# A mixture-of-experts stage whose TensorE order is written out by hand and pinned

## The chip, the cores and the metric

One core of a Trainium2 chip runs the whole program. The metric is the device time of one execution in microseconds; less is better. Three executions of the kernel before are at hand, and one more was recorded by the hardware profiler.

## The reference

The program is one transformer block on 1024 tokens of width 1024: a token mixer (differential attention and gated linear attention), a layer norm, and a hierarchical mixture of experts. Only the last is touched. Each token goes to two of 32 experts:

```
def expert_block(args):
    xblk, e = args
    h = jax.nn.silu(xblk @ wg[e]) * (xblk @ wu[e])
    return h @ wd[e]
...
y = jax.ops.segment_sum(yb.astype(jnp.float32) * buf_w[:, None], buf_tok, num_segments=n_tok + 1)[:n_tok]
```

`xblk` holds 128 gathered rows of one expert; a token's two results are weighted and added. Everything is float32. An expert has three matrices of 2 MB (`wg`, `wu`, `wd`), so 192 MB of weights are read once.

## The kernel before

`experts()` runs after the mixer. Expert 0 has a fixed place (`full32`). The other 31 are sorted by how many rows they got, and rank r has a fixed room: ranks 0 to 3 have 256 rows, 4 and 5 have 192, 6 and 7 have 128, 8 to 18 have 64, and 19 to 30 have 32. Ranks 0 to 7 are called large here, the 23 others small.

**Loads.** A matrix comes in two halves of 1 MB, each by one DMA on SyncE's queue (L332) into one of eight buffers, `raw0` to `raw7` (`NRAW`, L43), which are used in turn. SyncE issues in order: a load whose buffer isn't free holds up all loads behind it.

**Large experts** (`big`, L426) split each half into a high and a low part (`split`, L336: ScalarE casts at L343, VectorE subtracts at L344), which frees the raw buffer. The parts have three buffers each. The products run in the fast fp32r form, three for each 128 rows of a half's column (`mm3`, L412; two products for a group of 64 rows, whose high and low part lie side by side): two halves of `wg`, two of `wu` (called up 0 to up 3 below), then the hidden rows are transposed (the turn, L472) and multiplied with both halves of `wd` (down, L481).

**Small experts** (`small64` L517, `small32` L554) use the raw halves as they are, in plain fp32; 64 rows fill half of the array's columns and 32 rows a quarter, so that two or four products stand side by side. Their raw buffers are free only when the products that read them are done. They too have an up, a turn (L538, L573) and a down.

**Rows** are gathered from DRAM by indirect DMAs on GpSimd's queue (L371) into two buffers (`xg`), transposed on TensorE (L380) and copied out. GpSimd's queue also issues the stores of results (L487, L551, L587), in order.

**Order.** `big`, `small64` and `small32` are generators. `chain` (L639) strings them together, and L663 to L667 take three steps of the small ones for two steps of the large ones, whatever the size of the large one; the last three small experts come behind all else (L684). This is the order in which instructions are handed to the framework. Its planner then orders each engine's instructions by its own costs, and the resulting order is fixed in the program; so products of a large and a small expert alternate in short runs on TensorE. A loop for overflowing rows (L701) runs zero times here. After it, results are gathered and normalized.

Of the kernel before, what the change touches and what calls it, by code (L numbers as in the profile page):

```python
# [74 lines left out]
class Moe:  # L75
# [232 lines left out]
    def experts(self, wg, wu, wd, g2d, out, ln2_g, ln2_b, x1d):  # L308
# [4 lines left out]
        MM = nc.tensor.matmul  # L313
# [39 lines left out]
        pxs = wx.enter_context(tc.tile_pool(name="pxs", bufs=2, reuse_waits="tile", side="right"))  # L353
# [22 lines left out]
        def x_T(xg, nm):  # L376
            for h in range(2):
                pt = ptr.tile([128, 4, 128], F32, tag="tr", name=f"tr{nm}_{h}")
                for k in range(4):
                    nc.tensor.transpose(pt[:, k, :], xg[:, (h * 4 + k) * 128:(h * 4 + k + 1) * 128], ident)  # L380
                yield slice(h * 4, h * 4 + 4), pt
# [11 lines left out]
        def x_small(u, xg=None):  # L393
            if xg is None:
                xg = gather(idx[:, u:u + 1], f"u{u}")
            T = pxs.tile([128, 8, 128], F32, tag="xT", name=f"xT{u}")
            for s, pt in x_T(xg, f"u{u}"):
                V.tensor_copy(T[:, s, :], pt)
            return T

# [11 lines left out]
        def mm3(ps, x, w, k0, nk, s=slice(0, 512)):  # L412

            for k, (wh, wl) in enumerate(w, k0):
                terms = ((x[0], wh), (x[1], wh), (x[0], wl)) if len(x) == 2 else ((x[0], wh), (x[0], wl))
                for j, (a, b) in enumerate(terms):
                    MM(ps, a[:, k, :], b[:, s], start=k + j == 0, stop=k == nk - 1 and b is wl)

# [7 lines left out]
        def big(half, xs, ydst, st=nc.gpsimd, pool=None):  # L426


            X = xs()
            n = len(X)  # L430
            w = split(half(0, 0), pool)
            yield
            ps = [[None] * n, [None] * n]
            hs = []
            order = ((0, 0), (0, 1), (1, 0), (1, 1), (2, 0))
            for j, (m, q) in enumerate(order[:4]):
                after = split(half(*order[j + 1]), pool)
                for u in range(n):
                    if q == 0:
                        ps[m][u] = pgu.tile([128, 512], F32, tag="gu", name=("pg", "pu")[m])  # L440
                    mm3(ps[m][u], X[u], w, q * 4, 8)
                w = after
                if (m, q) == (0, 1):
                    for u in range(n):
                        if len(X[u]) == 1:
                            sg = halves(ps[0][u], "sgh", "sg", 4)
                            S.activation(sg, sg, AF.Silu)
                        else:
                            sg = px.tile([128, 512], F32, tag="sg", name="sg", bufs=4)
                            S.activation(sg, ps[0][u], AF.Silu)  # L450
                        hs.append(sg)
                if j < 3:
                    yield
            w += split(half(2, 1), pool)
            hT = []
            for u in range(n):
                if len(X[u]) == 1:
                    t = halves(ps[1][u], "uph", "ys", 2)
                    V.tensor_tensor(hs[u], t, hs[u], op=ALU.mult)
                    T = px.tile([128, 4, 128], F32R, tag="hH", name="h2")  # L460
                    H, L = T[:, :, 0:64], T[:, :, 64:128]
                    hT.append((T,))
                    m = 64
                else:
                    V.tensor_tensor(hs[u], ps[1][u], hs[u], op=ALU.mult)
                    H = px.tile([128, 4, 128], F32R, tag="hH", name="hH")
                    L = px.tile([128, 4, 128], F32R, tag="hL", name="hL")
                    hT.append((H, L))
                    m = 128
                pt = ptr.tile([128, 4, m], F32, tag="tr", name="trh")  # L470
                for k in range(4):
                    nc.tensor.transpose(pt[:, k, :], hs[u][:, k * 128:(k + 1) * 128], ident[0:m, 0:m])  # L472
                S.copy(H, pt)
                V.tensor_tensor(L, pt, H.bitcast(F32), op=ALU.subtract)
            yield
            for u in range(n):
                ys = px.tile([128, 1024], F32, tag="ys", name="ys")
                for c in range(2):
                    s = slice(c * 512, c * 512 + 512)
                    yp = py.tile([128, 512], F32, tag="y", name="yp")  # L480
                    mm3(yp, hT[u], w, 0, 4, s)  # L481
                    if len(X[u]) == 1:
                        t = halves(yp, "yh", "sg", 4)
                        V.tensor_tensor(ys[0:64, s], t, g2[0:64, s], op=ALU.mult)
                    else:
                        V.tensor_tensor(ys[:, s], yp, g2[:, s], op=ALU.mult)
                st.dma_start(ydst[u], ys if len(X[u]) == 2 else ys[0:64])  # L487
            yield

        def full32(raws, T, ydst):  # L490
# [8 lines left out]
            h = px.tile([128, 512], F32, tag="sg", name="hf", bufs=4)  # L499
# [3 lines left out]
            for k in range(4):  # L503
                nc.tensor.transpose(pt[:, k, :], h[:, k * 128:(k + 1) * 128], ident)
# [4 lines left out]
            for c in range(2):  # L509
                yp = py.tile([128, 512], F32, tag="y", name="ypf")  # L510
# [6 lines left out]
        def small64(r, half, xs, c0, p0):  # L517


            T = xs()  # L520
            yield
            ps = pgu.tile([128, 512], F32, tag="gu", name=f"ps{r}")
            for k in range(8):
                if k % 4 == 0:
                    a, b = half(0, k // 4)[0], half(1, k // 4)[0]
                x = T[:, k, c0:c0 + 64]
                s = slice((k % 4) * 512, (k % 4) * 512 + 512)
                MM(ps[0:64, :], x, a[:, s], start=k == 0, stop=k == 7)  # L528
                MM(ps[64:128, :], x, b[:, s], start=k == 0, stop=k == 7)  # L529
                if k == 3:  # L530
                    yield
            sg = px.tile([128, 512], F32, tag="sg", name=f"sg{r}", bufs=4)
            S.activation(sg[64:128, :], ps[0:64, :], AF.Silu)  # L533
            h = px.tile([64, 512], F32, tag="sg", name=f"h{r}", bufs=4)
            V.tensor_tensor(h, ps[64:128, :], sg[64:128, :], op=ALU.mult)
            pt = ptr.tile([128, 4, 64], F32, tag="tr", name=f"trh{r}")
            for k in range(4):
                nc.tensor.transpose(pt[:, k, :], h[:, k * 128:(k + 1) * 128], ident[0:64, 0:64])  # L538
            hT = px.tile([128, 4, 64], F32, tag="hH", name=f"hT{r}")
            V.tensor_copy(hT, pt)  # L540
            yield
            d = [half(2, 0), half(2, 1)]
            yp = pgu.tile([128, 512], F32, tag="gu", name=f"yp{r}")
            for k in range(4):
                for c in range(2):
                    o = (k % 2) * 1024 + c * 512
                    MM(yp[c * 64:c * 64 + 64, :], hT[:, k, :], d[k // 2][0][:, o:o + 512], start=k == 0, stop=k == 3)
            ys = px.tile([128, 512], F32, tag="ys", name=f"ys{r}")
            V.tensor_tensor(ys, yp, g2h, op=ALU.mult)
            for c in range(2):  # L550
                nc.gpsimd.dma_start(yd[p0:p0 + 64, c * 512:c * 512 + 512], ys[c * 64:c * 64 + 64, :])  # L551
            yield

        def small32(r, half, xs, c0, p0, st=nc.gpsimd):  # L554
            T = xs()
            yield
            ps = pgu.tile([128, 256], F32, tag="gu", name=f"ps{r}")
            for k in range(8):
                if k % 4 == 0:
                    ab = half(0, k // 4)[0], half(1, k // 4)[0]  # L560
                x = T[:, k, c0:c0 + 32]
                for g in range(4):
                    o = (k % 4) * 512 + (g % 2) * 256
                    MM(ps[g * 32:g * 32 + 32, :], x, ab[g // 2][:, o:o + 256], start=k == 0, stop=k == 7)  # L564
                if k == 3:
                    yield
            sg = px.tile([128, 256], F32, tag="sg", name=f"sg{r}", bufs=4)
            S.activation(sg[64:128, :], ps[0:64, :], AF.Silu)
            h = px.tile([64, 256], F32, tag="sg", name=f"h{r}", bufs=4)
            V.tensor_tensor(h, ps[64:128, :], sg[64:128, :], op=ALU.mult)  # L570
            pt = ptr.tile([128, 2, 64], F32, tag="tr", name=f"trh{r}")
            for k in range(2):
# [1053 lines left out]
```

## Time and profile before

| | us |
|---|---|
| median of 3 runs | 2104.81 (2104.39 to 2104.88) |
| the profiled execution | 2098.06 |
| its span, first to last instruction | 2096.3 |
| TensorE busy in the span | 1921.5 (92%) |
| VectorE busy | 1162.1 (55%) |
| ScalarE busy | 843.0 (40%) |
| GpSimd busy | 243.7 (12%) |

A view of the trace counts microseconds from the span's start. The experts' part begins at about 1418 us, when its first weights are asked for, and the last products of a small expert start at 2032 us. Busy time of TensorE includes the drain of each product, so that isolated products count for more than their share of a dense run; the distance from one start to the next says what a product costs in a run. "DMA share" is the mean busy share of the core's 16 DMA engines, and PEclk the granted clock, 1.00 being 2.4 GHz and 0.5 being 1.2 GHz.

### The profile page before, as it was taken

What the parts mean: (1) busy time and instruction counts of PE and PEld (TensorE: products, weight loads), DVE (VectorE), ACT (ScalarE), POOL (GpSimd) and SP (SyncE); (2) the same over time, 40 slices, a digit from 0 to 9 for tenths busy, and PEclk for the clock granted to TensorE, in tenths of its full rate; (3) what the DMA queues carried; (4) which work ended last, traced back from release to release, by engine and by line L of the source; (5) the groups of instructions that cost most, each with busy time, mean ns of one, the idle gap of its engine ahead of it and who ended that gap; (6) DMA issues with size and microseconds to landing.
All of it is one profiled execution on the core that took longest, in us unless ns stands there. A gap on an engine that the chain in (4) does not pass through costs nothing. (4 is left out here: it accounts for less than half of the span.)

```text
span 2096.3 us, 29039 instructions
## 1 busy us (share of the span) xinstructions
PE 1921.5 (92%) x11039; PEld 1364.9 (65%) x11039; DVE 1162.1 (55%) x2110; ACT 843.0 (40%) x1426; POOL 243.7 (12%) x353
## 2 busy tenths in 40 slices
PE   6999999999999999999989999885998999988856
PEld 4777777777777776777767778673664555544322
DVE  7655286657665754866726567875433333444315
ACT  4322166556655663655534335331321222232202
POOL 1131100000000000000010100411111101111015
PEclk9999999999999999999999999897999999999988
DMA  7896472221123121121286735409797999999996
GB/s 270 230 249 226 159 238 66 91 91 66 56 91 94 63 91 58 61 85 57 88 269 208 244 118 201 141 31 379 303 420 288 346 371 366 349 371 404 422 386 240
DMA packets 142541, 434.32 MB, mean 207 GB/s; under 512 B 19096, under 2 KB 48408, under 8 KB 116288
## 3 DMA queue, kind: packets, MB, share of 16 engines
q1 hardware_dynamic: 98176, 350.29, 45.6%
q0 software_dynamic: 42880, 81.82, 12.2%
q8 instruction: 87, 1.43, 0.3%
q10 hardware_dynamic: 1344, 0.34, 0.1%
q14 instruction: 54, 0.44, 0.1%
HBM read 359.51 MB, written 72.89 MB: 206 GB/s over the span
## 5 line engine op out<-in xcount | busy, mean ns | idle before, releaser
L1075 DVE CUSTOM_DVE_ANT_0 t<-sc,B 128x256 f32<-128x256 f32 (+7 forms) x128 | 95.9, 754 | 63.7 <-PE sc L1072 58.6
L344 DVE TENSOR_TENSOR wL<-rawr,wH 128x1024 fp32r<-128x1024 f32 x96 | 113.8, 1219 | 15.6 <-ACT wH L343 15.3
L854 PE MATMUL v<-wv,uH 128*128 128x512 f32 x256 | 101.4, 407 | 5.0 <-DVE veL L799 2.9
L1077 ACT ACTIVATE t<-t,nm 128x256 f32<-128x256 f32 (+7 forms) x128 | 98.7, 772 | 17.2 <-DVE nm L1075 16.9
L343 ACT CAST wH<-rawr 128x1024 fp32r<-128x1024 f32 x96 | 95.2, 1046 | 23.5 <-DMA rawr<-in_wd 10.2
L816 PE MATMUL g<-uH,wH_g 128*128 128x512 f32 x256 | 102.3, 400 | 1.8 <-DVE kz L1034 1.8
L855 PE MATMUL v<-wv,uL 128*128 128x512 f32 x256 | 101.9, 398 | 0.1
L817 PE MATMUL g<-uL,wH_g 128*128 128x512 f32 x256 | 101.8, 397 | 0.0
L818 PE MATMUL g<-uH,wL_g 128*128 128x512 f32 x256 | 101.7, 397 | 0.0
L856 PE MATMUL v<-wv,uH 128*128 128x512 f32 x256 | 101.7, 397 | 0.0
L528 PE MATMUL ps<-rawr,xT 128*64 128x512 f32 x176 | 82.1, 601 | 0.6 <-DMA rawr<-in_wg 0.6
L529 PE MATMUL ps<-rawr,xT 128*64 128x512 f32 x176 | 79.2, 597 | 0.7 <-DMA rawr<-in_wu 0.7
L798 ACT CAST aH<-pta 128x512 fp32r<-128x512 f32 (+1 forms) x80 | 43.4, 542 | 71.3 <-PE pta L1096 71.0
L1070 PE MATMUL sc<-sk,sq 128*128 128x512 f32 (+2 forms) x192 | 70.2, 370 | 1.2 <-DVE nm L1075 0.3
L799 DVE TENSOR_TENSOR aL<-pta,aH 128x512 fp32r<-128x512 f32 (+1 forms) x80 | 50.7, 634 | 34.8 <-ACT aH L798 33.8
L1082 DVE SCALAR_TENSOR_TENSOR t<-t,rsum,t 128x128 f32<-128x128 f32 (+3 forms) x64 | 52.2, 816 | 27.3 <-ACT t L1081 27.0
L1072 PE MATMUL sc<-kz,sq 128*128 128x512 f32 (+2 forms) x192 | 66.0, 350 | 0.0
L564 PE MATMUL ps<-rawr,xT 128*32 128x256 f32 x768 | 56.9, 399 | 9.8 <-DMA rawr<-in_wu 7.3
L533 ACT ACTIVATE sg<-ps 64x512 f32<-64x512 f32 x11 | 6.5, 590 | 146.7 <-PE ps L529 146.7
L854 PEld LDWEIGHTS v<-wv,uH 128*128 128x128 f32 x256 | 48.1, 190 | 24.4 <-ACT ve L861 5.2
L1386 PE MATMUL wba<-baH,wH_wba 128*128 128x512 f32 x128 | 50.7, 400 | 10.8 <-DVE gs L1392 10.3
L380 PE MATMUL tru<-ident,xgu 128*128 128x128 f32 x192 | 32.3, 305 | 29.9 <-DMA xgu<-u2d,idx 26.0
(538 smaller groups left out, 5259.5 us busy)
## 6 DMA issues: line engine op xcount, KB each, us to landing
rawr<-in_wg SPq DMA_DIRECT2D x62, 1024.0 KB, 10.0
rawr<-in_wu SPq DMA_DIRECT2D x62, 1024.0 KB, 8.8
rawr<-in_wd SPq DMA_DIRECT2D x62, 1024.0 KB, 12.3
war<-in_w_ada SPq DMA_DIRECT2D x32, 512.0 KB, 5.3
yd<-o SPq DMA_DIRECT2D x24, 512.0 KB, 6.6
wa<-in_w_ada_sc SPq DMA_DIRECT2D x8, 1024.0 KB, 4.7
wvr<-in_wv SPq DMA_DIRECT2D x32, 256.0 KB, 3.0
wr_g<-in_wgt SPq DMA_DIRECT2D x16, 512.0 KB, 4.6
```

The lines of the kernel that those rows point to most:

```text
L343: S.copy(H[:, s], raw[:, s])
L344: V.tensor_tensor(L[:, s], raw[:, s], H[:, s].bitcast(F32), op=ALU.subtract)
L528: MM(ps[0:64, :], x, a[:, s], start=k == 0, stop=k == 7)
L529: MM(ps[64:128, :], x, b[:, s], start=k == 0, stop=k == 7)
L816: MM(ps, H[:, k, :], uH[k][:, s], start=k == 0, stop=False)
L817: MM(ps, H[:, k, :], uL[k][:, s], start=False, stop=False)
L818: MM(ps, L[:, k, :], uH[k][:, s], start=False, stop=k == 7)
L854: MM(ps, uH[k][:, t], wv[c][k][:, 0, :], start=k == 0, stop=False)
L855: MM(ps, uL[k][:, t], wv[c][k][:, 0, :], start=False, stop=False)
L856: MM(ps, uH[k][:, t], wv[c][k][:, 1, :], start=False, stop=k == 7)
L1075: V.tensor_tensor_reduce(out=t[:, :n], in0=ps[:, :n], in1=B[:, 1024 - n:1024], scale=1.0, scalar=3e38, op0=ALU.add, op1=ALU.min, accum_out=nm)
L1077: S.activation(t[:, :n], t[:, :n], AF.Exp, bias=nm, scale=-1.0, accum_out=rsum[:, c:c + 1])
```

## The change

Every product and transpose of `experts()` is pinned behind the one that was traced before it, so that TensorE's order is the order of the program text. `big` becomes a class whose steps (`rows`, `split`, `up`, `turn`, `down`) are called one by one; the two small forms become one class `Small`. A small expert's up is a block that stands whole between two half matrices of a large expert, with all its six loads called just ahead; its turn stands inside the large expert's next product (`mid`), and its down at the start of the next block, behind which the next small expert's rows are gathered and transposed (`small_ahead`). Large experts get four blocks (256 rows), two (192 rows) or one (128 rows), and come in the order 0, 1, 6, 4, 5, 2, 3, 7. Half k+1 is split ahead of up k. Smaller edits: small experts' sums move from the four buffers `pgu` to the two of `py`, `full32`'s from `py` to `pgu`; small rows have one buffer for each of two sizes in place of two shared; `sg` has two buffers for four; `mm3` takes the low part of the weights first.

```
-        MM = nc.tensor.matmul
+        def MM(*a, **kw):
+            return tc.keep_in_program_order(nc.tensor.matmul(*a, **kw))
+        def transpose(*a):
+            return tc.keep_in_program_order(nc.tensor.transpose(*a))
...
-        pxs = wx.enter_context(tc.tile_pool(name="pxs", bufs=2, reuse_waits="tile", side="right"))
+        pxs = wx.enter_context(tc.tile_pool(name="pxs", bufs=1, reuse_waits="tile", side="right"))
...
-                terms = ((x[0], wh), (x[1], wh), (x[0], wl)) if len(x) == 2 else ((x[0], wh), (x[0], wl))
+                terms = ((x[0], wl), (x[0], wh), (x[1], wh)) if len(x) == 2 else ((x[0], wl), (x[0], wh))
...
+        class Big:
...
+            def up(self, k, mid=lambda: None):
+                m, q = self.order[k]
+                for u, X in enumerate(self.X):
                     if q == 0:
+                        self.ps[m, u] = pgu.tile([128, 512], F32, tag="gu", name=("pg", "pu")[m])
+                    mm3(self.ps[m, u], X, self.w[k][:2], q * 4, 8)
+                    if u == 0:
+                        mid()
+                    mm3(self.ps[m, u], X, self.w[k][2:], q * 4 + 2, 8)
...
+        class Small:
...
+            def load(self):
+                self.w = {k: self.half(*k)[0] for k in ((0, 0), (1, 0), (0, 1), (1, 1), (2, 0), (2, 1))}
+            def up(self, q):
...
+                    self.ps = py.tile([128, w], F32, tag="y", name=f"ps{self.r}")
...
+        large = [r for r in (0, 1, N192, N256, N256 + 1, 2, 3, N192 + 1)]
+        small = []
+        for n in range(max(N64 - N128, NS - N64)):
+            small += [r for r in (N64 + n,) if r < NS] + [r for r in (N128 + n,) if r < N64]
...
+        def small_block():
+            nonlocal last, turned
+            cur = ahead
+            late = last and not turned
+            if late:
+                turn()
+            elif last:
+                last.down()
+            cur.load()
+            if not queue:
+                behind_loads()
+            cur.up(0)
+            if late:
+                last.down()
+            cur.up(1)
+            last, turned = cur, False
+            small_ahead()
...
+        cur = placed(large[0])
+        cur.rows()
+        small_ahead()
+        cur.split(0)
+        cur.up(0)
+        cur.split(1)
+        for n, r in enumerate(large):
+            slots = 4 if r < N256 else 2 if r < N192 else 1
+            if slots > 1 and n:
+                small_block()
+            cur.split(2)
+            cur.up(1, turn)
+            if slots > 2:
+                small_block()
+            cur.split(3)
+            cur.up(2, turn)
+            if slots > 3:
+                small_block()
+            cur.split(4)
+            cur.up(3, turn)
+            nxt = placed(large[n + 1]) if n + 1 < len(large) else None
+            if nxt:
+                nxt.rows()
+            cur.split(5)
+            if nxt:
+                nxt.split(0)
+            small_block()
+            cur.turn()
+            if nxt:
+                nxt.up(0, turn)
+            elif ahead:
+                small_block()
+            cur.down()
+            if nxt:
+                nxt.split(1)
+            cur = nxt
+        while ahead:
+            small_block()
+        turn()
+        last.down()
```

## Rows read from the trace of the kernel before

**Rows 1.** The page's 40 slices of the span: TensorE's busy tenths, and GB/s moved.

```profile
PE   6999999999999999999989999885998999988856
...
GB/s 270 230 249 226 159 238 66 91 91 66 56 91 94 63 91 58 61 85 57 88 269 208 244 118 201 141 31 379 303 420 288 346 371 366 349 371 404 422 386 240
```

**Rows 2.** Five stretches: busy us (count) per engine; the last three columns: PEclk, DMA share, GB/s.

```profile
1434.00:1461.00 27.00, 25.43 (x84) 13.16 (x82) 20.10 (x49) 4.96 (x6) 0.59 (x1) 0.97 1.02 395
1461.00:1485.00 24.00, 15.57 (x72) 10.53 (x74) 8.68 (x10) 6.24 (x8) 5.06 (x5) 0.79 0.54 198
1485.00:1575.00 90.00, 88.23 (x544) 56.10 (x540) 34.22 (x45) 23.77 (x32) 11.77 (x18) 1.00 1.01 410
1575.00:1895.00 320.00, 293.82 (x1531) 163.75 (x1531) 122.71 (x159) 78.72 (x106) 37.33 (x54) 0.96 0.91 348
1895.00:2030.00 135.00, 108.91 (x768) 51.46 (x769) 45.11 (x65) 25.81 (x33) 14.52 (x26) 0.97 1.01 418
```

**Rows 3.** DMA of 1434 to 2034 us: the sum, and the gathers, with median landing.

```profile
DMA packets 35289, 221.94 MB, mean 370 GB/s; under 512 B 4790, under 2 KB 4790, under 8 KB 11272
...
xgu<-u2d,idx POOLq DMA_INDIRECT x23, 9.3
```

**Rows 4.** Timeline of SyncE's queue around 1470 us: start, us, what.

```profile
1458.15 0.33 SPq L332 DMA_DIRECT2D rawr<-in_wu  x1
1484.43 0.33 SPq L332 DMA_DIRECT2D rawr<-in_wg  x1
```

**Rows 5.** Timeline of TensorE: the first and the third gathered row block's transposes.

```profile
1469.43 1.94 PE L380 MATMUL tru<-ident,xgu 128*128 128x128 f32 x8 [9.15 <-DMA xgu<-u2d,idx]
...
1478.86 1.04 PE L380 MATMUL tru<-ident,xgu 128*128 128x128 f32 x8
```

**Rows 6.** Timeline of GpSimd: the third gather's issue.

```profile
1471.64 0.99 POOL L371 DMA_INDIRECT xgu<-u2d,idx  x1 [7.95 <-PE tru L380]
```

**Rows 7.** Timeline of TensorE: small experts' products (64 rows down, 32 rows up, 64 rows up).

```profile
1494.04 3.65 PE L547 MATMUL yp<-rawr,hT 128*64 128x512 f32 x16
...
1503.34 3.66 PE L564 MATMUL ps<-rawr,xT 128*32 128x256 f32 x64
...
1984.09 0.59 PE L529 MATMUL ps<-rawr,xT 128*64 128x512 f32 x1
...
1984.52 0.59 PE L529 MATMUL ps<-rawr,xT 128*64 128x512 f32 x1
```

**Rows 8.** Timeline of TensorE: large products behind a small expert's.

```profile
1624.38 0.51 PE L417 MATMUL pg<-wL,xH 128*128 128x512 f32 x1
1624.72 0.40 PE L417 MATMUL pg<-wH,xH 128*128 128x512 f32 x1
1624.96 0.39 PE L417 MATMUL pg<-wH,xL 128*128 128x512 f32 x1
```

**Rows 9.** Timeline of TensorE behind two waits (idle before, in brackets).

```profile
1575.38 0.50 PE L417 MATMUL yp<-wH,hL 128*128 128x512 f32 x1 [1.73 <-DVE hL L474]
...
1576.46 0.63 PE L417 MATMUL yp<-wH,hL 128*128 128x512 f32 x1
1576.88 0.63 PE L417 MATMUL yp<-wL,hH 128*128 128x512 f32 x1
...
1976.34 0.50 PE L417 MATMUL yp<-wH,hH 128*128 128x512 f32 x1 [1.62 <-ACT wH L343]
1976.68 0.39 PE L417 MATMUL yp<-wH,hL 128*128 128x512 f32 x1
```

**Rows 10.** Waits of 1469 to 2034 us, GpSimd's and TensorE's longest: total, times, longest.

```profile
POOL xgu L371 <- PE tru L380: 175.4, 19, 27.8
...
PE tru L380 <- DMA xgu<-u2d,idx: 14.1, 2, 9.2
```

**Rows 11.** The page's groups: the two halves of a split, mean ns behind the busy time.

```profile
L344 DVE TENSOR_TENSOR wL<-rawr,wH 128x1024 fp32r<-128x1024 f32 x96 | 113.8, 1219 | 15.6 <-ACT wH L343 15.3
...
L343 ACT CAST wH<-rawr 128x1024 fp32r<-128x1024 f32 x96 | 95.2, 1046 | 23.5 <-DMA rawr<-in_wd 10.2
```

## The forecast, made before the change was run

> **What bounds the kernel now.** I read the slices first, then stretches, then the DMA queues, and single instructions last. The slices show TensorE at nine tenths nearly everywhere, which would make it the bound [rows 1]; the line of GB/s speaks for another: the last third moves 288 to 422 where the mixer mostly stays under 100. So the experts' part has two candidates, and their work must be counted.
>
> TensorE's work: in a dense run a large product starts every 0.23 to 0.24 us [rows 8]; there are 12 groups of 128 rows with 72 products each and 2 groups of 64 with 48, 960 in all, so 221 us. A small expert of 64 rows has 16 pairs in its up, a pair every 0.43 us, and 3.6 us of down: 10.5 us, times 11 is 115. One of 32 rows has 3.6 us of up and, with half as many products, 1.8 of down [rows 7]: 5.4 us, times 12 is 65. Transposes (23 gathers of 8, a little under 1 us each [rows 5]; 124 of hidden rows) are some 30 us. Together 430 us. The profile shows 491 us of TensorE busy between 1485 and 2030 alone [rows 2]: the rest is drains and refills where the two kinds of product alternate (0.34 us to the next start behind a change in place of 0.24, [rows 8]) and stretches at half clock.
>
> The DMA engines' work: 221.94 MB from 1434 to 2034 us [rows 3]. Between 1895 and 2030 they move 418 GB/s at a share of 1.01, between 1485 and 1575 410 [rows 2]. At 418 the whole takes 531 us; it took 600. So the DMA engines are the nearer bound, and 69 us are lost to them: 54 in the 320 us from 1575 to 1895, at 348 GB/s in place of 418 (320 x (1 - 348/418)), and 13 in the 24 us from 1461 to 1485, at 198. In the first of these TensorE is busy for 294 of 320 us: there both wait for each other, because the order gives a large expert of 256 rows the same two and a half small ones as one of 128. The end, where TensorE has little to do, is left bare to the DMA engines.
>
> **The change, part by part.** *The ratio.* A cycle of a 256-row expert with its four blocks (two of either size): TensorE 4 ups of 24 products and 48 of down, 33 us; blocks 32; transposes, turns and changes of kind about 9; together 74. DMA: 30 loads of 1.05 MB at 418 GB/s, 2.5 us each, 75; three to four gathers and the stores, 8; together 83. A cycle of 192 rows with two blocks: TensorE 18 + 9 + 16 + 6 = 49, DMA 45 + 5 = 50. One of 128 rows: 28 against 34. So the DMA engines are the longer ones in every cycle, barely so at 192 rows. If their queue never ran dry, the 54 us would come back: this is the first term, **-54**; nothing, if 348 GB/s were all that the engines can do in such a mix, but they did 418 for 135 us and 410 for 90 [rows 2], so I take the whole. The Trainium skill (DMA: Bandwidth & Descriptors, Where 436 GB/s comes from) says that HBM holds a core's reads to about 358 GB/s, with 435 as the limit of the fabric. By that the first term would be 320 x (1 - 348/358) = 9 us and the sum 2125; the trace doesn't agree, with its 418.
>
> *Does it run dry?* A load waits for the buffer of the eighth before it. In a block, TensorE takes loads nearly as they land, and its two down halves keep two buffers until the next block; six loads, 15 us, remain queued behind them. Between two blocks there is mostly one large half (24 products, 5.5 us) and 3.6 us of down, 9 us, well inside 15. The exception is the block ahead of a large down: behind it come the turn (1.5 us), the next expert's up 0 (5.5), the down (11), then half of the small down (1.8) until a buffer is free, with 1 us to launch: 21 us, against 15 of queued loads and 2 for what is still landing. That leaves 3.5 to 4 us of hole; for four cycles 14. With 192 rows it is 18 against 17, but TensorE has no slack there; I take 4 us, twice, 8. With 128 rows, 13 against 17: none. Sum **+22**; bounds 0 (stores of results fill the hole) and 47 (below).
>
> *The start.* Before, the tenth load is issued at 1458.15 and the next at 1484.43, when a small expert's first products free a buffer [rows 4]. After, eleven loads go ahead, but TensorE must take the rows of ranks 0 and 19 first. Ready at 1469.43 [rows 5], it does two row blocks to 1474, then waits for the third gather, which can't be issued before 1471.64 [rows 6] and whose transposes ran at 1478.86 [rows 5]; two ups of 5.5 us and a first small half of 1.8 follow, to about 1493.5. That is 9 us later, less 2.5 for the eleventh load: **+6.5**; +2 if the gather lands with the second's transposes at 1474, +9 if the eleventh load brings nothing.
>
> *Pinning.* Every wait of TensorE now holds up all behind it: products, so raw buffers and SyncE's loads; sums, so ScalarE and VectorE; results, so GpSimd's stores and the gathers behind them. A gather lands 9.3 us after its issue [rows 3], and GpSimd stood 175 us on the two row buffers; TensorE waited 14 us for gathers, in two goes [rows 10]. After, a late gather stops TensorE by some 3 to 6 us, some ten times; between blocks six queued loads cover it. I take nothing; without cover 30 us, in the range. Sixteen transposes in a row wait for two PSUM buffers, 2.5 us a large expert, counted in the 9 above.
>
> *The rest at nothing:* a small turn waits about 1.4 us for silu and product, and 6 large products, 1.4 us, stand ahead of it. Low part first: a product waits for VectorE's 1.2 us behind ScalarE's 1.0 [rows 11], but a half is split a block ahead of its use; bare, 48 halves would cost 1.2 us each. Fewer buffers for sums, `sg` and small rows: each is read out before its next use, a block later. Fewer changes of kind, each 0.1 us [rows 8], save TensorE time that isn't on the path. The last expert's loads, sums and stores are as before.
>
> **Sum.** 2098.1 - 54 + 22 + 6.5 = 2073 for an execution like the profiled one. The median of the runs stands 6.7 us above that one, so **2080**.
>
> **Rivals.** *No holes* (a store or a gather always queued): 2058. For it: 1485 to 1575, ups and a down of a 256-row expert among small ones, ran at 410 [rows 2]. Against: 21 us against 17.
>
> *Half of it*: gathers and holes together take 40 us in place of 22: 2098. For it: the row buffers' 175 us [rows 10]. With 47 us, and the start, nothing is left: 2105, no change.
>
> *Slower by the clock.* Behind a wait of 1.73 us products started every 0.42 us, half speed; behind one of 1.62 us they didn't fall [rows 9]. Pinned, TensorE waits for weights ahead of most blocks. If half the blocks' products ran at 1.2 GHz, a 256-row cycle would need 74 + 16 = 90 us against 83 and a 192-row one 57 against 50: 4 x 7 + 2 x 7 = 42 us and longer holes, 2125. It decides once about a third of the blocks' products run so. Against it: in the bare end TensorE waits for loads as well and is granted 0.97 [rows 2]. The Trainium skill (TensorE: Matmul & The Clock Gate, HAM oscillation) tells of this trap, a kernel whose short groups of products each wait for a DMA and each start cold. The rows show both outcomes.
>
> *At its limit already*: the DMA engines could do no better here, and only the later start is new: 2111. The 418 of [rows 2] speaks against it. This is what the skill's 358 would lead to, but for the 9 us.
>
> **How the numbers follow.** Chances: the forecast, 2064 to 2092, 0.48; no holes, below that, 0.10; half, 2092 to 2101, 0.13; no change, within 0.2% (4 us, about what a measurement here can tell), 0.07; slower by the clock 0.17; at its limit 0.05. So faster 0.71, same 0.07, slower 0.22. The range 2054 to 2122 leaves out the far ends of no holes (0.06) and of the clock (0.11).
>
> **What would show it.** Right: GB/s over 400 from 1500 us to the end, but for short dips ahead of each large down; loads resuming at about 1493; the last weights near 2008 in place of 2033; fewer changes of kind on TensorE. Wrong: a PEclk under 0.9 over many stretches; SyncE waiting for small downs while the DMA share falls below 0.9; TensorE waiting for gathers for over 30 us; VectorE or ScalarE standing on a split whose half hasn't landed, with a sum waiting behind it.

## The result, and the profile after

The changed kernel takes 2121.5 us (median of four runs, 2120.8 to 2125.0) against 2104.6 for the kernel before in the same comparison: a ratio of 1.0089, 95% interval 1.0072 to 1.0105. It is slower; the forecast was 2080 and faster.

The changed kernel's profiled execution has a span of 2123.1 us. The page's slices (compare [rows 1]): TensorE's busy tenths, the granted clock in tenths, the DMA engines' busy share, GB/s.

```profile
PE   6999999999999999999979999866898888988776
...
PEclk9999999999999999999989999887999999999888
DMA  7896472231123222121386736229799887999886
GB/s 270 220 241 228 160 235 65 90 100 55 55 90 100 67 78 58 72 80 56 116 277 189 233 122 211 100 89 359 297 375 420 325 355 308 372 401 394 326 360 237
```

The same five stretches as [rows 2], same columns. The experts' part began 7.5 us later in this execution than in the one of before (first weights asked for at 1425.46 against 1417.96; the mixer is the same, and over the eleven other profiles below this moment lies anywhere from 1418 to 1427), so they stand a little earlier in the work.

```profile
1434.00:1461.00 27.00, 21.73 (x66) 11.47 (x67) 18.01 (x51) 4.51 (x6) 0.00 (x0) 0.84 1.02 389
1461.00:1485.00 24.00, 10.33 (x43) 6.67 (x42) 9.00 (x12) 4.79 (x7) 4.97 (x5) 0.69 0.83 332
1485.00:1575.00 90.00, 83.99 (x511) 53.95 (x512) 29.43 (x40) 17.62 (x24) 11.74 (x17) 0.93 0.80 317
1575.00:1895.00 320.00, 269.88 (x1554) 157.51 (x1552) 124.46 (x159) 83.70 (x113) 36.96 (x55) 0.93 0.90 367
1895.00:2030.00 135.00, 113.16 (x667) 66.86 (x666) 48.13 (x61) 28.27 (x35) 11.69 (x20) 0.92 0.90 366
```

In the 320 us that were to bring the gain the rate rose only from 348 to 367 GB/s, and the share didn't rise at all (0.91, then 0.90). On both sides of them, where the kernel before moved 410 and 418 GB/s at a share of 1.01, it fell to 317 and 366. TensorE is busy *less* (270 us of 320 where it was 294) at a lower clock. So neither engine is the bound throughout; each waits for the other. The windows of the eight longest lulls of the loads say how (same columns):

```profile
1560.00:1564.00 4.00, 4.00 (x43) 2.43 (x41) 0.87 (x2) 0.00 (x0) 0.55 (x1) 1.00 0.07 25
1648.00:1660.00 12.00, 11.04 (x61) 8.76 (x63) 11.42 (x12) 10.33 (x13) 1.60 (x2) 1.00 0.21 71
1715.00:1723.00 8.00, 8.00 (x63) 5.75 (x62) 5.49 (x8) 5.03 (x7) 1.03 (x1) 1.00 0.10 22
1752.00:1756.00 4.00, 4.00 (x20) 2.00 (x20) 2.73 (x4) 1.10 (x2) 0.00 (x0) 1.00 0.50 203
1776.00:1788.00 12.00, 9.76 (x67) 6.51 (x65) 8.99 (x11) 6.59 (x9) 3.26 (x2) 0.86 0.23 74
1818.00:1824.00 6.00, 6.00 (x28) 3.55 (x28) 1.38 (x2) 0.00 (x0) 1.16 (x2) 1.00 0.29 84
1909.00:1913.00 4.00, 4.00 (x20) 1.99 (x20) 0.69 (x1) 0.00 (x0) 0.54 (x1) 1.00 0.06 23
1996.00:2008.00 12.00, 12.00 (x55) 8.97 (x55) 10.24 (x11) 8.38 (x9) 0.54 (x1) 1.00 0.23 71
```

In seven of them the DMA engines do next to nothing (a share of 0.06 to 0.29), in the one at 1752 half of what they can. TensorE works on meanwhile: without a pause at full clock in six, and for 11.0 and 9.8 of 12 us in those at 1648 and 1776. Taken as length times (1.01 - share), they lose 3.8, 9.6, 7.3, 2.0, 9.4, 4.3, 3.8 and 9.4: 49.6 us. What stops the loads is in SyncE's queue around the second lull: start, us, what; the two issues of the merged second row are 29 us apart.

```profile
1631.67 0.33 SPq L337 DMA_DIRECT2D rawr<-in_wd  x1
1632.49 29.25 SPq L337 DMA_DIRECT2D rawr<-in_wg  x2
1661.99 0.71 SPq L337 DMA_DIRECT2D rawr<-in_wu  x1
```

And on TensorE's timeline in the same place, from the end of one small up to the small down that belongs to it (idle before in brackets); the last line is from a later place, for comparison:

```profile
1629.67 2.78 PE L315 MATMUL ps<-rawr,xT 128*32 128x256 f32 x28 [1.94 <-DMA rawr<-in_wu]
1632.38 1.86 PE L318 MATMUL trh<-ident,sg 128*128 128x128 f32 x8
...
1637.34 0.39 PE L315 MATMUL yp<-wL,hH 128*128 128x512 f32 x1
...
1656.57 1.03 PE L318 MATMUL tru<-ident,xgu 128*128 128x128 f32 x8
1658.57 1.25 PE L318 MATMUL tru<-ident,xgu 128*128 128x128 f32 x8 [0.96 <-DVE xL L395]
1659.75 1.93 PE L315 MATMUL yp<-rawr,hT 128*32 128x256 f32 x32
...
1668.26 1.97 PE L315 MATMUL ps<-rawr,xT 128*64 128x512 f32 x2 [6.58 <-DMA rawr<-in_wg]
...
1722.57 1.07 PE L315 MATMUL ps<-rawr,xT 128*64 128x512 f32 x2
```

The small expert's up is done at 1632.4. Its turn stands inside the next large up, and its hidden rows are ready soon after; but its down, whose products free two raw buffers, stands in the next block. Rank 6 (128 rows) follows rank 1, and gets one block only, behind its up 3. So the down waits for the turn, rank 6's up 0, the 48 products of rank 1's down and rank 6's other three ups: 27.3 us. SyncE's queue, in order, waits with it, and when the buffers are free TensorE stands 6.6 us until the next weights land, and falls to half clock (the two `ps` products take 1.97 us; at 1722.57, at full clock, the first two of another such expert take 1.07). The waits over the whole part: SyncE's queue for products of a small down (`yp`) or a small up (`ps`), then TensorE's for weights and for rows, then GpSimd's; the last two compare with [rows 10] (total us, times, longest).

```profile
SPq L337 <- PE yp L315: 267.4, 38, 23.6
SPq L337 <- PE ps L315: 141.7, 62, 29.3
...
PE ps L315 <- DMA rawr<-in_wu: 39.0, 20, 5.5
PE ps L315 <- DMA rawr<-in_wg: 23.3, 8, 6.6
PE tru L318 <- DMA xgu<-u2d,idx: 13.5, 2, 11.1
...
POOL xgu L376 <- PE tru L318: 154.3, 19, 22.0
```

SyncE's queue in the kernel before, for splits, small ups (L528, L529, L564) and small downs (L547, L583):

```profile
SPq L332 <- DVE wL L344: 142.8, 42, 7.1
SPq L332 <- PE ps L528: 83.7, 17, 8.0
SPq L332 <- PE ps L564: 79.2, 22, 6.5
SPq L332 <- PE yp L547: 60.4, 22, 11.5
SPq L332 <- PE ps L529: 49.7, 22, 25.8
SPq L332 <- PE yp L583: 27.8, 15, 5.1
```

Its waits for small downs came to 88 us, none over 11.5; after the change they come to 267, the longest 23.6. The total alone says little, because a wait costs nothing while loads called earlier still run: the fastest version below waits 159 us for small downs and has the DMA engines at a share of 1.01. It is the long waits that use these loads up.

**Where the 17 us are.** Each row is one profiled execution. From SyncE's and TensorE's timelines of each profile: (a) from the first experts' load to the load at which the queue resumes after its first long stop, (b) from there to the last load of a `wd` half, (c) from there to the end of the last small down; and, for (b), the time lost against 418 GB/s, its length times (1 - GB/s / 418). All in us, GB/s and share over (b).

| kernel | a | b | c | a+b+c | GB/s | share | lost in b |
|---|---|---|---|---|---|---|---|
| before | 66.5 | 532.5 | 17.7 | 616.8 | 374 | 0.95 | 56 |
| after | 76.3 | 540.3 | 18.1 | 634.8 | 369 | 0.91 | 63 |
| e1_down_early | 76.4 | 505.0 | 18.9 | 600.3 | 392 | 0.96 | 31 |
| e2_block_first | 61.2 | 554.8 | 23.4 | 639.3 | 362 | 0.90 | 74 |
| e3_unpinned | 71.4 | 546.7 | 18.0 | 636.1 | 364 | 0.91 | 71 |
| e4_ratio_alone | 65.9 | 531.8 | 19.2 | 616.9 | 375 | 0.96 | 55 |
| e7_down_all | 76.5 | 478.1 | 18.9 | 573.6 | 414 | 1.01 | 5 |
| e9_down_all_first | 61.6 | 494.3 | 19.2 | 575.1 | 407 | 0.99 | 13 |
| e10_raw7 | 76.1 | 579.2 | 10.7 | 665.9 | 351 | 0.87 | 93 |
| e8_filler | 76.3 | 536.3 | 18.4 | 631.1 | 372 | 0.91 | 59 |
| e11_all_unpinned | 71.7 | 544.8 | 18.0 | 634.5 | 364 | 0.93 | 70 |
| e12_all_even | 76.4 | 481.6 | 16.7 | 574.7 | 412 | 1.00 | 7 |

The change cost 9.9 us in (a), 7.8 in (b), 0.3 in (c): 18.0, against 17 between the medians. (The two profiled executions differ by 26.8; 7.5 of that is the later start of the experts' part.) In (b) it was to gain some 32.

### The profile page after: what moved, and what is told of

The parts are those of the page before. It is cut to its first block, busy times and chain, and to the rows that moved or that the text cites. A ratio compares the mean times of both kernels' runs of the same rounds, so it can differ in the third digit from the quotient of the medians.

```text
span 2123.1 us, 29031 instructions
## 1 busy us (share of the span) xinstructions
PE 1914.3 (90%) x11039; PEld 1377.8 (65%) x11039; DVE 1162.8 (55%) x2110; ACT 842.9 (40%) x1426; POOL 244.3 (12%) x353
## 5 line engine op out<-in xcount | busy, mean ns | idle before, releaser
L315 PE MATMUL ps<-rawr,xT 128*32 128x256 f32 (+1 forms) x1120 | 159.7, 498 | 62.2 <-DMA rawr<-in_wu 39.0
L315 PEld LDWEIGHTS ps<-rawr,xT 128*32 128x32 f32 (+1 forms) x1120 | 54.4, 129 | 164.3 <-issue 65.8
L561 ACT ACTIVATE sg<-ps 64x256 f32<-64x256 f32 (+1 forms) x23 | 11.0, 479 | 288.8 <-PE ps L315 288.8
L563 DVE TENSOR_TENSOR h<-ps,sg 64x256 f32<-64x256 f32 (+1 forms) x23 | 12.7, 554 | 142.0 <-ACT sg L561 141.8
L1134 DVE SCALAR_TENSOR_TENSOR t<-t,rsum,t 128x128 f32<-128x128 f32 (+3 forms) x64 | 52.2, 816 | 27.3 <-ACT t L1133 27.0
L315 PE MATMUL yp<-rawr,hT 128*32 128x256 f32 (+1 forms) x560 | 64.9, 461 | 2.0 <-SPq L746 1.5
L1124 PE MATMUL sc<-kz,sq 128*128 128x512 f32 (+2 forms) x192 | 65.9, 350 | 0.0
## 6 DMA issues: line engine op xcount, KB each, us to landing
rawr<-in_wu SPq DMA_DIRECT2D x62, 1024.0 KB, 14.5
```

Of the source, the lines that this page charges most:

```text
L315: return tc.keep_in_program_order(nc.tensor.matmul(*a, **kw))
```

## The experiments

The theory after the comparison: the block's two down halves hold two of eight raw buffers for so long that SyncE's queue runs dry. Rivals: TensorE's half clock behind each wait is the loss; the pins are; the ratio is what one should keep. Ratios are to the kernel before, run on the same chip beside each, with 95% intervals.

**One early down.** Ahead of each large down, the small down is called first.

```
             if nxt:
                 nxt.up(0, turn)
+                last.down()
+                last = None
```

> The changed kernel, but the small expert's down is called right behind the next large expert's up 0, ahead of the large down. Theory 1 (a block's two down halves keep two of the eight raw buffers until the next block, so SyncE and then the DMA engines stand at every large down; some 50 us are lost at these eight places): the buffers come free 11 us earlier, the lost time falls by about 30 us, 2085 to 2095. Theory 2 (TensorE, pinned and half the time at 1.2 GHz behind its waits, is the bound): its work and its waits stay, 2115 to 2122.

Measured: 2085.4, ratio 0.9913 (0.9890 to 0.9936): 36 us less than the change, with two lines added. It is the same TensorE work at the same sizes, and (b) is 35 us shorter. That is the first theory's range; the second theory's 2115 to 2122 is out. Of the long lulls only those at the two experts of 192 rows are left, each between its two blocks: 102 GB/s at a share of 0.29 from 1700 to 1716, and 120 at 0.33 from 1760 to 1776. The clock isn't excluded by this run: with the lulls gone it rose too, from 0.93 to 0.95 over (b).

**A block ahead of the first large up**, to bring the loads back sooner.

```
-        cur.rows()
         small_ahead()
+        cur.rows()
         cur.split(0)
-        cur.up(0)
+        small_block()
+        cur.up(0, turn)
```

> The changed kernel, but the first small expert's rows are gathered first and its block stands ahead of the first large expert's up 0. Theory 1 with the start as a term of its own: loads resume some 17 us earlier, with nine loads ahead in place of eleven, so 12 us less, and one block fewer at the end, 3 us: 2106 to 2112. Theory 2: later waits take the gain back, 2117 to 2122.

Measured: 2121.1, ratio 1.0081 (1.0052 to 1.0110), the same as the change and in the second theory's range. The loads do resume 15 us sooner, (a) is 61.2, though with nine loads ahead of the stop in place of eleven; (b) and (c) take it back, 14.5 and 5.3. So the late start wasn't worth its microseconds here.

**Without the pins**, the rest of the change as it is (`MM` and `transpose` without `keep_in_program_order`).

> The changed kernel without the pins: same text, TensorE's order by the planner. Theory 1 (the place of the down in the text does the harm): the planner may move some small downs ahead, most stay, 2105 to 2120. Theory 3 (the pins themselves do the harm, since any late gather, split or load stops all products): the harm goes and the better ratio of small to large stays, 2070 to 2095.

Measured: 2120.2, ratio 1.0079 (1.0056 to 1.0102), the upper end of the first theory's range. The pins are not what made the change slower.

**The ratio alone**, in the kernel before: the small steps dealt out by weights 4, 2 and 1, and the large experts' order.

```
-        heavy = list(range(N128))
+        heavy = [0, 1, N192, N256, N256 + 1, 2, 3, N192 + 1]
+        wt = [4 if r < N256 else 2 if r < N192 else 1 for r in heavy for _ in range(5)]
...
-            while done < nl and done * nh < (j + 1) * nl:
+            while done < nl and done * sum(wt) < sum(wt[:j + 1]) * nl:
```

> The kernel before, with only the order of the large experts (0, 1, 6, 4, 5, 2, 3, 7) and the share of small steps for each (4, 2 or 1 by its size) taken over; still planned, not pinned. If the first term of the forecast was right (the even ratio gives back most of 54 us): 2060 to 2080. If the ratio is worth little, because both engines wait for each other through the buffers anyway: 2095 to 2110.

Measured: 2100.0, ratio 0.9996 (0.9979 to 1.0014). Taken alone, the ratio is worth nothing.

**Every small down behind the large up that holds its turn.**

```
+        def down():
+            nonlocal last
+            if last and turned:
+                last.down()
+                last = None
...
             cur.up(1, turn)
+            down()
...
             cur.up(2, turn)
+            down()
...
             cur.up(3, turn)
+            down()
...
                 nxt.up(0, turn)
+                down()
```

> The change, with every small down taken out of the next block and put right behind the large up in which its turn stood, at every place and not only ahead of a large down. First theory (a small expert's two down buffers are held until the next block, so SyncE's queue runs dry): the 11 us holes that are left at the two 192-row ranks, where two ups stand between blocks, go too, 22 us beside the one-place version's 2085: 2062 to 2072. Second theory (what was won there was TensorE's time, fewer stretches at half clock, not the buffers): the small down is the same work at the same clock, 2083 to 2090; each small down now stands alone between large products, which costs up to 23 changes of kind of 0.1 us.

Measured: 2059.1, ratio 0.9797 (0.9776 to 0.9817), the fastest with the next one, and faster than both kernels by over 40 us. That is 3 us below the first theory's range and far from the second's. It is called the fast version below. Its stretch of 320 us (columns as [rows 2]):

```profile
1575.00:1895.00 320.00, 295.88 (x1813) 179.23 (x1812) 136.07 (x175) 89.10 (x121) 41.94 (x64) 0.97 1.01 415
```

SyncE's queue waiting for products of a down (total us, times, longest):

```profile
SPq L337 <- PE yp L315: 159.2, 38, 11.0
```

415 GB/s at a share of 1.01 where the change had 367 at 0.90, and no wait for a `yp` over 11 us; the waits that are left, 159 us in all, cost the DMA engines next to nothing. On TensorE, the small expert of the lull above ends its up at 1628.0 and has its down at once behind the up 0:

```profile
1625.02 2.96 PE L315 MATMUL ps<-rawr,xT 128*32 128x256 f32 x28 [2.68 <-DMA rawr<-in_wu]
1627.91 1.68 PE L318 MATMUL trh<-ident,sg 128*128 128x128 f32 x8
1630.91 0.33 PE L318 MATMUL trh<-ident,h 64*128 64x64 f32 x2
1632.77 1.93 PE L315 MATMUL yp<-rawr,hT 128*32 128x256 f32 x32
```

**The same with a block ahead of the first up** (both edits above, and a `down()` behind the first up 0).

> The same, with a first small block ahead of the first large up, and its rows gathered first. That start alone won nothing on top of the change. First theory: there its lead was lost again in the holes and the tail; with the holes gone the DMA engines are busy throughout and the lead of 7 to 12 us should show, 2053 to 2065. Rival: the lead is lost at the end in any case, since one small block fewer is left behind the last large expert: 2062 to 2072, as without it.

Measured: 2059.6, ratio 0.9793 (0.9771 to 0.9814). That lies in the first theory's range and below the rival's, but so does the fast version with its 2059.1, and beside that one no lead shows. So the rival is right that the lead is lost, but not in where: (c) is 19.2, 18.9 without; the 15 us won in (a) are lost again in (b), 16. About 5 of these are two loads: nine stand ahead of the stop here, eleven in the fast version, and a load is 2.5 us. Another 4 or 5 are lost in one place, from 1788 to 1816, at 318 GB/s and a share of 0.81 (385 and 0.97 in the fast version).

**Seven raw buffers** (`NRAW = 7`) in the change.

> The change with seven raw buffers in place of eight, nothing else. First theory: with one load less in flight each of the seven long holes and the start come 2.5 us sooner and last as much longer, and short ones appear ahead of the 192-row blocks: 2138 to 2150. Rival (the DMA engines or TensorE's own work bound the changed kernel, the queue's depth doesn't): 2119 to 2126.

Measured: 2147.8, ratio 1.0211 (1.0190 to 1.0233): 26 us for one buffer, as the first theory had it. The depth of the queue is among what sets the time of the changed kernel.

**Products to fill TensorE's waits** in the change, ahead of fourteen small ups; `FILL` has 3 to 17 of them for each, by the wait seen there.

```
+                if q == 0:
+                    f = self.T.rearrange("p a b -> p (a b)")
+                    for _ in range(FILL.get(self.r, 0)):
+                        MM(ps[:, 0:256], f[:, 0:128], f[:, 0:256], start=True, stop=True)
```

> The change with idle products (of rows already there, into the sums' own buffer, overwritten by the first real product) put ahead of the fourteen small ups in which TensorE waited for weights, as many as fill the wait seen there; so TensorE is kept from standing still and should not fall to half clock behind these waits. It adds products whose results are thrown away. First theory (the waits come from the queue, and the clock is a consequence worth little): the holes stay, 2115 to 2124. Second theory (the half clock behind the waits is what made the change slower: 58 us busy at half clock against 27 before, so 15 us of TensorE's time, and longer holes through it): 2098 to 2108.

Measured: 2117.6, ratio 1.0075 (1.0054 to 1.0095), within the first theory's range. Its stretches of 320 and 135 us:

```profile
1575.00:1895.00 320.00, 295.22 (x1723) 188.45 (x1720) 124.12 (x159) 83.93 (x112) 36.87 (x55) 0.98 0.90 367
1895.00:2030.00 135.00, 127.55 (x779) 79.89 (x779) 47.07 (x60) 26.54 (x34) 11.66 (x20) 1.00 0.91 369
```

The clock is back at 0.98 and 1.00 (it was 0.93 and 0.92), and the DMA columns are those of the change: 0.90 and 367. So TensorE's waits bring the half clock, and the half clock doesn't bring the lulls. Its price is the difference of the two ratios, (1.0089 - 1.0075) x 2102 = 3 us, and by both intervals together not over 9; the 15 that the second theory asked for aren't there. The added products may have delayed some real ones, which would hide a part of the gain; but behind them TensorE still waits for weights in 18 places, 17.5 us in all, so they ended in time there.

**The fast version without the pins.**

> The version with every small down behind its large up, without the pins: the planner orders TensorE by its own costs again, from the same program text. First theory (the order of the text and the buffers' turn decide; the pins alone do nothing, as they did nothing in the change itself): 2055 to 2066. Rival (with the holes gone the pinned order is what keeps the loads coming; the planner would move the small downs back behind large products): 2075 to 2100.

Measured: 2117.7, ratio 1.0070 (1.0044 to 1.0097). The first theory fails here, by 52 us above its range. The rival has the direction right, but its range ends 18 us too low, and its reason isn't what the trace shows, as the waits below say. The planner's order on TensorE, at the same place (one small up in pieces among a large one's products):

```profile
1624.25 1.07 PE L315 MATMUL ps<-rawr,xT 128*32 128x256 f32 x4
...
1627.08 0.40 PE L315 MATMUL pg<-wH,xH 128*128 128x512 f32 x1
...
1627.64 1.92 PE L315 MATMUL ps<-rawr,xT 128*32 128x256 f32 x28
```

SyncE's queue over (b):

```profile
SPq L337 <- PE ps L315: 216.4, 61, 26.4
SPq L337 <- DVE wL L349: 131.6, 43, 8.5
SPq L337 <- PE yp L315: 101.1, 36, 7.1
```

The planner takes a block apart, and the loss in (b) is 70 us again. The small downs do come early, the longest wait for one is 7.1 us; it is the ups, spread among large products, for which the loads wait more (216.4 us; 135.4 in the fast version). That these waits make the whole loss was not tested. The pins by themselves bring nothing (the change with and without them: 1.0089 and 1.0079); an order that frees buffers early brings nothing unless it is kept; the two together bring 57 to 61 us (0.9797 against 1.0070, 1.0079 and 1.0089). So how long the other buffers of a block are held counts as much as when its down comes.

**The fast version with a nearly even ratio**: three blocks for 256 and 192 rows, two for 128.

```
-            slots = 4 if r < N256 else 2 if r < N192 else 1
+            slots = 3 if r < N192 else 2
```

> The same version, pinned, with three blocks to a large expert of 256 or 192 rows and two to one of 128, in place of four, two and one: nearly the even ratio of the kernel before, but in blocks. First theory (the ratio was never what held the DMA engines back; they are the longer ones in every cycle with either ratio, so with the buffers freed in time they run throughout): 2057 to 2067. Rival (the forecast's first term: TensorE is the longer one at 256 rows and idles at 128 when the ratio is even): 2080 to 2105.

Measured: 2061.7, ratio 0.9813 (0.9800 to 0.9825). The ratio of 4, 2 and 1 is worth next to nothing in blocks either: the two intervals overlap.

## Why the prediction was wrong

**The bound** was named rightly: the DMA engines, at about 418 GB/s, were held back by waits. The fast version moves 414 GB/s over 478 us. The Trainium skill (DMA: Bandwidth & Descriptors, Where 436 GB/s comes from) has HBM hold a core's reads to about 358; this row doesn't agree with it, and the rival that followed from it (2111) is out. That the prediction's other sum by this figure of the Trainium skill, 2125, lies near the measured time is chance, for the limit that it rests on isn't there.

**The first term, -54 for the ratio, failed in its cause, not its size.** The loss in (b) fell from 56 to 5 us in the fast version, so 51 were there to win. But they weren't lost to the ratio: it moved nothing in the kernel before, and with a nearly even one the fast version loses 7. The prediction itself worked out that the DMA engines are the longer ones in every cycle, "barely so at 192 rows", and then gave the ratio the credit. The runs show that the gain comes from buffers freed in time in an order that is kept.

**The holes, +22, are the step that decided.** It rests on "Between two blocks there is mostly one large half" and on four like holes of 256 rows ("for four cycles 14"), and both are wrong by the program's own order. The sign that the prediction named for it is there: SyncE waits for small downs, up to 23.6 us and 267 in all (88 before), and the DMA share is at or below 0.9. Where the prediction placed holes, it sized them well: four of 256 rows were given 3.5 to 4 us each, and the two that are followed by a large expert with a block of its own at once took 3.8 and 3.8; the two of 192 rows were given 4 each and took 2.0 and 4.3. What it missed is when the *next* block comes. Behind ranks 1 and 3 comes an expert of 128 rows, which has no block until its up 3: three more ups, and holes of 9.6 and 9.4. ("With 128 rows, 13 against 17: none" holds for the block of rank 6 itself, behind which no lull is among the eight.) And ranks 4 and 5 have three ups between their two blocks: holes of 7.3 and 9.4, to which it gave nothing. With these the term is 49.6, near its own outer bound of 47. The first early down (ahead of large downs) and the fast version (everywhere) each took out the holes of its places.

With 49.6 the sum would have been 2098.1 - 54 + 49.6 + 6.5 = 2100, and 2107 by the medians. The other 14 us of the loss in (b), 63.3 - 49.6, lie outside these windows. By the share over (b), 540.3 x (1.01 - 0.91) / 1.01 = 53 us are idle engines, so some 4 of the 14 are small lulls, and the other 10 slower transfer while busy.

**The start, +6.5.** Right as a mechanism: the loads resumed at 1501.80, 76.3 us after the first load (forecast 1493.5, or 75.5 after that of before). It is 9.9 later than before, less the same 2.5 for an eleventh load, 7.4.

```profile
1470.06 0.33 SPq L337 DMA_DIRECT2D rawr<-in_wg  x1
1501.80 0.33 SPq L337 DMA_DIRECT2D rawr<-in_wu  x1
```

But a start 15 us sooner changed no time in either version that tried it. Part of that was no lead, but two loads left for later, 5 us. With the holes gone, another 4 or 5 went in the one lull from 1788; the rest is open.

**Pinning at nothing** held for what was asked, late gathers: TensorE waited 13.5 us for them, in two goes, 14.1 before [rows 10]. Its cover failed elsewhere: pinned, a small product waits for weights in place of letting large ones pass, 62 us in 28 waits. And its gain was overlooked, since nothing in the forecast asked what the planner would do with a good order.

**Slower by the clock**, 2125, ends nearest to the measured time of the rivals, and is wrong. The granted clock did fall, to 0.92 to 0.93 in the last three stretches, but the sign that it named, under 0.9 over many, isn't there: only the first two short stretches are below that. The Trainium skill (TensorE: Matmul & The Clock Gate, HAM oscillation) describes products that each start cold behind a DMA wait, and the trace agrees for the `ps` at 1668.26, behind 6.58 us (1.97 us for what takes 1.07 at full clock). The filled waits show the price here, about 3 us. "No change", 2105, had the right size at 0.07, 47 us, but put a part of it down to gathers.

**The rest at nothing** can't be told apart in these runs, but the fast version contains all of these edits and runs with the DMA engines at 1.01, so none of them is in its way. Fewer changes of kind came as forecast: TensorE goes from a large product to a small one or back 43 times in the experts' part, 175 times before (counted in the traces from 1400 to 2070 us). What the kernel before lost its 56 us to was not taken apart by a run of its own. Like the two unpinned versions, which lose 70, it has the planner's order, and SyncE's waits have the same make-up as in the unpinned fast version: 212.6 us for small ups, 142.8 for splits, 88.2 for small downs there, 216.4, 131.6 and 101.1 here.

## What to carry over

Where one in-order queue feeds a few buffers, work out for each buffer how long it is held, from the landing to the last product that reads it. Walk the order to the *next* place where it is released, through every branch of the loop, not the typical one; a hole is that time less what the loads already queued take. Move the consumer that frees the buffer, not the work that is long. And an order that frees buffers in time is only worth something if it is the one that runs: test it with and without the scheduler's freedom.

## What the runs showed of the hardware

The rate of the DMA engines is not their share times a constant. In the kernel before they moved 374 GB/s at a share of 0.95 (394 for a full share), in the unpinned fast version 364 at 0.93 (391), in the pinned one 414 at 1.01 (410), and in the change 369 at 0.91 (405). By the table, the four runs in the planner's order have 391 to 400 for a full share over (b), the eight pinned ones 402 to 412. So of the 56 us lost before, only 533 x (1.01 - 0.95) / 1.01 = 32 are idle engines; the rest is slower transfer while busy. It isn't bound to the planner's order throughout: the last 135 us before ran at 418 and 1.01 [rows 2]. Why it is slower wasn't measured.
